# A decoder block in fp32 on one core: load order behind the gate products, and the combination of attention groups in four pieces

## The chip, the core and the metric

The kernel runs on one core of a Trainium2 chip. The core has five engines with instruction queues of their own: PE (matrix products), DVE and POOL (elementwise work), ACT (activation functions and copies), and SP, which here only issues transfers. ACT and POOL can issue transfers too. The metric is the device time of one execution in microseconds; lower is better. A profiled execution adds a trace of every instruction.

## The reference

The block computes, for x of 2048 tokens and 1024 channels:

```
h      = rmsnorm(x) * gain
proj   = h @ w_in                       # 5376 columns: q, k, v, u, z, gate_a, gate_b
y_attn = softmax-combination over 3 dilation groups of windowed attention (256 columns)
u, z   = gelu(proj_u), gelu(proj_z)     # 512 columns each
y_gmlp = u * (w_spatial @ layernorm(z) + b_spatial)      # per chunk of 128 tokens
merged = sigmoid(gate_a) * (y_attn @ w_branch_attn) + sigmoid(gate_b) * (y_gmlp @ w_branch_gmlp)
x      = x + rmsnorm(merged @ w_out)
x      = x + rmsnorm(relu(rmsnorm(x) @ w_mlp_in)**2 @ w_mlp_out)
```

The combination of the three attention groups, for each token and head, takes the running maxima and denominators of the groups, forms three weights that add to one, scales the three group outputs by them and adds them up.

## The kernel before

**Arithmetic.** Every fp32 operand of a large product is split into a rounded high part and a rest (`split`, L67), and one product is three matmuls: high by high, high by rest, rest by high (`mm3`, L94). The 2048 tokens are four chunks c of 512; half 0 is chunks 0 and 1, half 1 is chunks 2 and 3.

**Stages around the change.** After q, k and v have been computed and stored, a generator (`filler`, L761) supplies matrix products in small steps, and other work is laid between its steps. One step of a plain product is one `mm3` for one of eight slices of the contraction. The filler's queue is: u and z of half 1, the gates (`gates`, L664), then z of half 0. Gates and the rest of u are computed by a seven-product scheme over both halves. Its list `seq` has phases; a product is twelve matmuls in four steps. The last phase has ten products, for half 0, and starts at index LAST. Each product needs one piece of weights, loaded four products ahead (`piece`) and split by POOL three products ahead (`split_piece`); each result is stored to DRAM one product later (`out_`).

During the gates the 48 units of attention are laid between the steps. When they are through, 75 more steps of the gates remain. Between these steps lie the combinations of chunks 2 and 3; those of chunks 0 and 1 lie between the steps of z of half 0. `combine` (L955) is a generator: it loads the three groups' rows of a chunk (A for chunks 2 and 3; one buffer, cw, for chunks 0 and then 1), does the arithmetic on DVE and ACT, and then PE transposes the result (L990), ACT evacuates it (L993) and SP stores it to the DRAM tensor ya_d (L994). The calls `combined((steps, k), ...)` say how many steps of the filler pass before the next piece of combination k; k counts the chunks in the order 2, 3, 0, 1.

**z of half 0.** It reads hT_b0 and then hT_b1 (the normalised input of chunks 0 and 1, split, reloaded from DRAM by `reload_h`, eight loads each of 512 KB) and the two tiles w_z0 (reloaded from wz_d, four loads of 1024 KB, `want(5)`). One chunk is four blocks of tokens of eight steps each; ACT applies Gelu to each block (L572), DVE takes its statistics (L574), and at the end of a chunk normalises it (L579). The branch weights wb are six tiles, each loaded into one of two raw buffers, its high part split by POOL and its rest by DVE (`split_in`). `spatial` loads the spatial weights into memory that the gates' result tiles (ga) held.

**The merge.** After z the branch products start: `load_y(2)` loads the six operand tiles yt of chunk 2 (two from ya_d, four from yg_d) and POOL splits them; `early_gates` loads gate values and the first output weights; `merge` (L1139) runs, for each of eight column blocks, six and twelve matmuls into two banks, which DVE multiplies by the gates (L1153). The spatial products of chunks 0 and 1 (`sz_out`, L546) lie behind the first two column blocks. Then `out_block` multiplies by w_out.

**What sets the order.** PE's order is the program's. The order of the other engines is chosen when the kernel is built, by a planner that models the run and takes, for each engine, the ready instruction that comes first in the program. `behind()` (L175) pins what is written inside it behind the last instruction written so far on ACT, DVE, POOL and SP. At run time each queue is strictly in order: an instruction that waits holds all that stand behind it, transfers on SP included.

Two lists rule the places that matter here: in `gates`, `ins` holds loads, of which one is issued after each product; and in the last phase `reload_h(0)` is put into `ins`, while the loads of w_z0 are issued together at index LAST + 2:

```
            if t == LAST + 2:
                want(5)
            ...
            for _ in range(2 if half and i == 4 else 1):
                if ins:
                    sp.dma_start(*ins.pop(0))
```

The six branch weights are issued ahead of z of half 0, and hT_b1's eight loads together where z begins (L780).

Of the kernel before, what the change touches and what calls it, by code (L numbers as in the profile page):

```python
# [41 lines left out]
def block_kernel(ctx, tc, a, out):  # L42
# [100 lines left out]
    ya_d = dtile([2, P, S], "yad")  # L143
# [443 lines left out]
    def want(q):  # L587
        if q < len(queue) and q not in loaded:
            wi, kind, n, half = queue[q]
            if kind == "z":  # L590
                if half and not n:
                    loaded[q] = load_wide(wi, "w_z1")
                    for kk in range(2):
                        sp.dma_start(wz_d[kk], f32(loaded[q][kk]))
                elif not n:
                    loaded[q] = wide_tiles("w_z0")
                    for kk in range(2):
                        for o in range(2):
                            sp.dma_start(f32(loaded[q][kk])[:, o], wz_d[kk][:, o])
            else:  # L600
                loaded[q] = load_w(wi, f"w_{kind}{n}{half}")

# [61 lines left out]
    def gates():  # L664
# [12 lines left out]
        for t, (half, i, n) in enumerate(seq):  # L677
            if t in starts:
                ph, t0 = starts[t], t
                if ph + 1 < len(phases):  # L680
                    s = (ph + 1) % 2
                    if not slots[s]:
                        slots[s] = hp.tile([P, 2, 2, 4, 512], F32R, name="opA", tag="hT", bufs=2)
                    for j, i2 in enumerate(phases[ph + 1][1]):
                        new = operand(phases[ph + 1][0], i2, slots[s][:, j])
                        ins += new[0]
                        todo += new[1]
                else:
                    ins += reload_h(0)
            elif todo and (t - t0) % 3 == 1 and t > t0 + 1:  # L690
                w, k = todo.pop(0)
                with behind():
                    split(w[:, 0, k:k + 2], w[:, 1, k:k + 2], f32(w)[:, 1, k:k + 2], "act", "pool")
            if t == LAST + 2:
                want(5)
            piece(t + PIECES)
            split_piece(t + SPLITS)
            if i in (1, 6, 5, 4):
                bank[n] = psum_mm(f"g{half}{i}{n}")
            p, w, h = bank[n], g_["w"].pop(t), g_["b"][half, i]  # L700
            for k in range(4):
                for m, (l, r) in enumerate(((0, 0), (0, 1), (1, 0))):
                    pe.matmul(p, w[:, l, k], h[:, r, k], start=i in (1, 6, 5, 4) and not k and not m,  # L703
                              stop=k == 3 and m == 2, skip_group_check=True)
                if (t, k) == (3, 2) and late:
                    sz_out(*late.pop(0))
                yield
            if t == 3:
                a = [ga.tile([P, 512], F32, name=f"ga{n_}", tag=f"ga{n_}", bufs=1) for n_ in range(12)]
                xs += a[:7]  # L710
                zs += a[7:9]
                vs = a[9:11]
                g_["vs"] = vs + xs[8:] + zs[8:]
                g_["raws"] += a[11:] + vs + zs[8:]
            x, z, fn = xs[n], zs[n], AF.Copy if n < 8 else AF.Gelu_apprx_tanh
            while out_:
                sp.dma_start(*out_.pop())
            for _ in range(2 if half and i == 4 else 1):
                if ins:
                    sp.dma_start(*ins.pop(0))  # L720
            if i == 1:
                act.activation(x, p, AF.Copy)
            elif i == 2:
                act.activation(z, p, fn)
                o = z, 0, 0
            elif i == 6:
                dve.tensor_add(z, x, p)
            elif i == 7:
                dve.tensor_add(x, x, p)
            elif i == 5:  # L730
                if (half, n) == (0, 0):
                    g_["vs"] = a[9:11]
                v = g_["vs"].pop(0)
                g_["vs"].append(v)
                dve.tensor_add(v, x, p)  # L735
                o = v, 1, 1
            elif i == 3:
                dve.tensor_add(z, z, p)
                o = z, 0, 1
            else:  # L740
                dve.tensor_add(x, x, p)
                o = x, 1, 0
            if n > 7 and i in (5, 3, 4):
                act.activation(o[0], o[0], fn)
            if i in (2, 5, 3, 4):
                c, dst = 2 * half + o[2], gate_d if n < 8 else u_d
                out_.append((dst[n % 8 * 2 + o[1], :, c * 512:(c + 1) * 512], o[0]))
# [13 lines left out]
    def filler():  # L761

        for q, (wi, kind, n, half) in enumerate(queue):
            if kind == "z" and n == 1:
                continue
            if kind == "g":
                yield from gates()
                cw.append(wp.tile([P, 4096], F32, name="cw", tag="w", bufs=3))
                next(cs[2])
                continue  # L770
            want(q)
            if kind == "u":
                want(q + 1)
            if (kind, n) == ("u", 1):
# [1 line left out]
            w = loaded[q]  # L776
            if kind == "z":
                if not half:
                    for z in reload_h(1):
                        sp.dma_start(*z)  # L780
                for ci in range(2):
                    yield from paced(z_chunk(zps[half], w, half * 2 + ci))
                    if half and not ci:
                        gates_ahead()
                continue
# [6 lines left out]
                    sp.dma_start(u_d[n * 2 + m, :, c * 512:(c + 1) * 512], t)  # L792

    fill = filler()
    cw, cs = [], []

    def steps(n):
        for _ in range(n):
# [156 lines left out]
    def combine(c):  # L955
# [18 lines left out]
        dve.reciprocal(M, M)  # L974
        for g in range(3):
            dve.tensor_mul(E[:, :, g, :], E[:, :, g, :], M)
        for i in range(4):
            for j in range(4):
                o = A[:, i, 0, j * 64:(j + 1) * 64]
                act.activation(o, o, AF.Copy, scale=E[:, i, 0, j:j + 1])  # L980
        for g in range(1, 3):
            o = A[:, :, g, 0:256].rearrange("p i (j e) -> p i j e", j=4)
            dve.tensor_tensor(o, o, widen(E[:, :, g, :], 64), op=OP.mult)
        dve.tensor_add(A[:, :, 1, :256], A[:, :, 1, :256], A[:, :, 2, :256])
        dve.tensor_add(A[:, :, 0, :256], A[:, :, 0, :256], A[:, :, 1, :256])
        yield
        for m in range(2):
# [3 lines left out]
            yt = cb.tile([P, 512], F32, name=f"ya_{c}{m}", tag="cya", bufs=2) if c > 1 else \  # L991
                st.tile([P, 512], F32, name=f"ya_{c}{m}", tag="ev", bufs=3)
            act.activation(yt, pt, AF.Copy)  # L993
            sp.dma_start(ya_d[m, :, c * 512:(c + 1) * 512], yt)  # L994
        yield

    units = [(g, c, j) for g in range(3) for c in range(4) for j in range(4)]
# [53 lines left out]
            with behind():  # L1051
                next(cs[k])

    combined((0, 0), (4, 1), (16, 0), (18, 0), (0, 1), (20, 1))
    steps(75 - 58)
    ec.close()
    ega.close()

    e2r = ExitStack()
    wbp = stack(e2r, "wbp", 1, side="right")  # L1060
    wb = [wbp.tile([P, 2, D], F32R, name=f"wb{k}") for k in range(6)]
    for k in range(6):
        raw = wp.tile([P, D], F32, name=f"wbraw{k}", tag="raw", bufs=2)
        split_in(wb[k], a["w_branch"][:, k, :], raw)
    ez = ExitStack()
    zps[0] = stack(ez, "zp0", 1, side="right")
    sg = spatial(zps[0], 0)
    next(sg)
    combined((14, 2), (14, 2), (1, 3), (14, 3))
    steps(5)  # L1070
    next(sg)
    combined((10, 3))
    run(fill)
    e1.close()

# [966 lines left out]
```

## Time and profile before

| | |
|---|---|
| median of 3 runs | 2671.59 us (2671.57 to 2674.1) |
| the profiled execution | 2670.21 us |
| its span, first to last instruction | 2668.5 us |
| PE busy | 2622.1 us, 98% of the span |
| DVE, ACT, POOL busy | 1650.0, 1090.5, 1192.3 us |
| mean granted PE clock | 0.992 |
| z of half 0 on PE | from 1014.57 to 1076.5 us |
| first merge on PE | from 1076.5 to 1132.9 us |

How such rows are read. A timeline row is: start in us, duration in us, engine (SPq and ACTq are the queues as they issue transfers), source line, operation, output<-input by the program's names, shape, count, and in brackets the idle time before it with the engine or transfer that ended it. A wait row is: who waited, at which line, for whom: total us, times, longest us. A row of a stretch is: from:to, length, busy us and instruction count of PE, of PE's weight loads, of DVE, ACT and POOL, the granted PE clock, the mean busy share of the 16 transfer engines, and GB/s. A transfer row is: output<-input, queue, count, KB each, median us from issue to landing. Ends of matmuls are modelled; starts are what to go by.

### The profile page before, as it was taken

The numbers are of one execution on the slowest core, as the hardware profiler recorded it, in microseconds if no ns is written. First come the engines' busy times: TensorE is split into PE (matmuls) and PEld (weight loads), VectorE is DVE, ScalarE is ACT, GpSimd is POOL, SyncE is SP. The second block draws the span as 40 slices with busy tenths as digits, with TensorE's granted clock in tenths as the row PEclk, the third lists the DMA queues.
The fourth block names the chain that finished last, engine by engine and source line by source line (L and its number), as shares of the span: only waits on it lengthen the run. The fifth ranks groups of instructions, "written<-read, shape, count | busy, mean of one in ns | idle before, by whom it ended". The sixth has DMA issues, their size and how long they took to land. (4 is left out here: it accounts for less than half of the span.)

```text
span 2668.5 us, 35509 instructions
## 1 busy us (share of the span) xinstructions
PE 2622.1 (98%) x12458; PEld 2188.0 (82%) x12458; DVE 1650.0 (62%) x2793; ACT 1090.5 (41%) x2281; POOL 1192.3 (45%) x1089
## 2 busy tenths in 40 slices
PE   9999999999999997899999999999999999999998
PEld 8888888888888876688888888888888888888887
DVE  5676675534533454665676665655537888888866
ACT  5213111254455333344445545655545333233334
POOL 0363354375464542310233564223315776676645
PEclk9999999999999998899999999999999999999999
DMA  8779768988888887643666464653343212222235
GB/s 321 281 248 320 270 226 293 300 286 256 289 271 241 240 294 285 228 167 137 208 225 256 135 227 152 214 155 121 110 151 111 87 60 83 87 87 87 87 111 213
DMA packets 389284, 528.29 MB, mean 198 GB/s; under 512 B 57009, under 2 KB 242097, under 8 KB 387570
## 3 DMA queue, kind: packets, MB, share of 16 engines
q1 hardware_dynamic: 301488, 438.13, 49.5%
q0 software_dynamic: 14992, 51.65, 5.1%
q10 hardware_dynamic: 72626, 36.25, 4.5%
q8 instruction: 98, 1.61, 0.2%
q14 instruction: 80, 0.66, 0.1%
HBM read 342.77 MB, written 183.17 MB: 197 GB/s over the span
## 5 line engine op out<-in xcount | busy, mean ns | idle before, releaser
L1893 PE MATMUL ya<-T_spots,s 128*128 128x512 f32 x1176 | 289.2, 389 | 0.7 <-ACT T_spots L70 0.5
L70 ACT ACTIVATE s<-sraw 128x768 fp32r<-128x768 f32 (+1 forms) x184 | 127.2, 696 | 330.2 <-POOL sraw L1694 156.2
L1893 PEld LDWEIGHTS ya<-T_spots,s 128*128 128x128 f32 x1176 | 220.5, 188 | 47.3 <-ACT T_spots L70 0.9
L78 DVE TENSOR_TENSOR s<-sraw,s 128x512 fp32r<-128x512 f32 x172 | 184.4, 1097 | 8.6 <-ACT s L70 7.2
L1366 PE MATMUL aa<-B,A 128*128 128x512 f32 x768 | 182.4, 390 | 0.7 <-DVE A L85 0.7
L1337 POOL TENSOR_TENSOR s<-w1r 128x512 f32<-128x512 f32 x32 | 42.3, 1323 | 308.6 <-DVE S L78 271.0
L703 PE MATMUL g<-opA,spots 128*128 128x512 f32 x672 | 171.8, 400 | 2.5 <-DVE cv L735 2.5
L1366 PEld LDWEIGHTS aa<-B,A 128*128 128x128 f32 x768 | 143.8, 188 | 31.3 <-DVE A L85 1.1
L703 PE MATMUL g<-opB,spots 128*128 128x512 f32 x648 | 164.7, 398 | 1.7 <-POOL spots L78 1.0
L1893 PE MATMUL yc<-T_spots,s 128*128 128x512 f32 x624 | 159.6, 389 | 0.0
L95 PE MATMUL x<-hT_a,wq 128*128 128x512 f32 x384 | 149.7, 390 | 0.0
L96 PE MATMUL x<-hT_a,wq 128*128 128x512 f32 x384 | 149.4, 389 | 0.0
L97 PE MATMUL x<-hT_a,wq 128*128 128x512 f32 x384 | 149.4, 389 | 0.0
L703 PEld LDWEIGHTS g<-opA,spots 128*128 128x128 f32 x672 | 122.0, 190 | 25.0 <-issue 2.9
L78 POOL TENSOR_TENSOR spots<-gr,spots 128x512 fp32r<-128x512 f32 x98 | 128.1, 1310 | 23.0 <-PE g L703 8.3
L1893 PEld LDWEIGHTS yc<-T_spots,s 128*128 128x128 f32 x624 | 117.1, 188 | 24.3
L703 PEld LDWEIGHTS g<-opB,spots 128*128 128x128 f32 x648 | 117.0, 189 | 23.9 <-POOL spots L78 1.8
L70 ACT ACTIVATE hl<-r 128x512 fp32r<-128x512 f32 x48 | 30.4, 633 | 235.4 <-POOL r L321 89.0
L72 POOL TENSOR_SCALAR spots<-gr 128x512 fp32r<-128x512 f32 x86 | 53.9, 627 | 142.8 <-PE g L703 105.6
L951 DVE TENSOR_REDUCE o<-po 128x256 f32<-128x512 f32 x48 | 33.2, 691 | 132.5 <-PE po L950 132.5
L1693 POOL TENSOR_TENSOR sraw<-sraw 128x256 f32<-128x256 f32 x56 | 41.9, 748 | 161.4 <-DVE s L78 158.4
L78 POOL TENSOR_TENSOR T_spots<-w2r,T_spots 128x512 fp32r<-128x512 f32 x70 | 104.5, 1520 | 7.3 <-ACT T_spots L70 7.3
(422 smaller groups left out, 6959.6 us busy)
## 6 DMA issues: line engine op xcount, KB each, us to landing
w1r<-in_w_mlp_in_dram SPq DMA_DIRECT2D x64, 512.0 KB, 3.6
sraw<-sd SPq DMA_DIRECT2D x128, 256.0 KB, 3.2
qk<-hl SPq DMA_DIRECT2D x24, 1024.0 KB, 5.5
qq<-qk SPq DMA_DIRECT2D x96, 256.0 KB, 5.2
w2r<-in_w_mlp_out_dram SPq DMA_DIRECT2D x16, 1024.0 KB, 7.8
sd<-u ACTq DMA_DIRECT2D x63, 256.0 KB, 3.5
g<-gated SPq DMA_DIRECT2D x58, 256.0 KB, 3.9
gr<-sgd SPq DMA_DIRECT2D x53, 256.0 KB, 4.8
```

The lines of the kernel that those rows point to most:

```text
L70: act.activation(hi, src, AF.Copy)
L72: pool.tensor_scalar(hi, src, 1.0, 1.0, op0=OP.mult, op1=OP.mult)
L78: (pool if lo_eng == "pool" else dve).tensor_sub(lo, src, f32(hi))
L95: pe.matmul(ps, lh, rh, start=start, stop=False)
L96: pe.matmul(ps, lh, rl, start=False, stop=False)
L97: pe.matmul(ps, ll, rh, start=False, stop=stop)
L703: pe.matmul(p, w[:, l, k], h[:, r, k], start=i in (1, 6, 5, 4) and not k and not m, stop=k == 3 and m == 2, skip_group_check=True)
L951: dve.tensor_reduce(ot[:, :, j * 64:(j + 1) * 64], po.rearrange("p (b h e) -> p b e h", b=4, h=2), axis=AX.X, op=OP.add)
L1337: pool.tensor_add(s1, a21, a22)
L1366: pe.matmul(p, w[:, l, k, :], h[:, r, k, :], start=i in (1, 6, 5) and not k and not n, stop=k == 3 and n == 2, skip_group_check=True)
L1693: pool.tensor_add(a22, a21, a22)
L1893: pe.matmul(p, s[:, l], w[r], start=i in (1, 2, 5) and not m and not o, stop=m == 1 and o == 2, skip_group_check=True)
```

## The change

Six edits that belong together.

1. `want(5)` no longer issues the four loads of w_z0 but returns them. At the start of the last phase they are put into `ins` with the eight loads of hT_b0, in the order two of w_z0, four of hT_b0, two of w_z0, four of hT_b0. One is issued after each of the ten products, two after the second and the third.
2. `combine` yields twice more: loads; weights of the groups; scaling; sums; transposes, evacuation and store. The places of the pieces between the steps are written anew. Chunk 2's first arithmetic is at step 18 (20 before), its transposes at 36 (38); chunk 3's transposes at 56 (58).
3. The stores to ya_d are issued by ACT's queue, not SP's.
4. The branch weights are not issued ahead of z but one every sixth step in it, from the sixth to the thirty-sixth.
5. The eight loads of hT_b1 are put into a list, `zin`, and issued one per step from the start of z.
6. In z, the pieces of chunk 0's combination stand at steps 12, 14, 17 and 24 after the step in which cw's loads are written, those of chunk 1 at 24 (loads), 38, 40, 43 and 52. The preparation of the spatial weights' row sums stands at 48.

```diff
                 elif not n:
                     loaded[q] = wide_tiles("w_z0")
-                    for kk in range(2):
-                        for o in range(2):
-                            sp.dma_start(f32(loaded[q][kk])[:, o], wz_d[kk][:, o])
+                    return [(f32(loaded[q][kk])[:, o], wz_d[kk][:, o]) for kk in range(2) for o in range(2)]
...
                 else:
-                    ins += reload_h(0)
+                    ws, hs = want(5), reload_h(0)
+                    ins += ws[:2] + hs[:4] + ws[2:] + hs[4:]
...
-            if t == LAST + 2:
-                want(5)
...
-            for _ in range(2 if half and i == 4 else 1):
+            for _ in range(2 if half and i == 4 or t in (LAST + 1, LAST + 2) else 1):
...
             if kind == "g":
                 yield from gates()
+                want(q + 1)
                 cw.append(wp.tile([P, 4096], F32, name="cw", tag="w", bufs=3))
                 next(cs[2])
                 continue
-            want(q)
+            if q not in loaded:
+                want(q)
...
                 if not half:
-                    for z in reload_h(1):
-                        sp.dma_start(*z)
+                    zin.extend(reload_h(1))
...
         for g in range(3):
             dve.tensor_mul(E[:, :, g, :], E[:, :, g, :], M)
+        yield
         for i in range(4):
...
             dve.tensor_tensor(o, o, widen(E[:, :, g, :], 64), op=OP.mult)
+        yield
         dve.tensor_add(A[:, :, 1, :256], A[:, :, 1, :256], A[:, :, 2, :256])
...
             act.activation(yt, pt, AF.Copy)
-            sp.dma_start(ya_d[m, :, c * 512:(c + 1) * 512], yt)
+            act.dma_start(ya_d[m, :, c * 512:(c + 1) * 512], yt)
...
-    combined((0, 0), (4, 1), (16, 0), (18, 0), (0, 1), (20, 1))
-    steps(75 - 58)
+    combined((0, 0), (4, 1), (14, 0), (4, 0), (4, 0), (10, 0), (2, 1), (4, 1), (4, 1), (10, 1))
+    steps(75 - 56)
...
-    for k in range(6):
+
+    def load_wb(k):
         raw = wp.tile([P, D], F32, name=f"wbraw{k}", tag="raw", bufs=2)
         split_in(wb[k], a["w_branch"][:, k, :], raw)
...
     next(sg)
-    combined((14, 2), (14, 2), (1, 3), (14, 3))
-    steps(5)
-    next(sg)
-    combined((10, 3))
+    while not cw:
+        steps(1)
+    todo = {12: (2,), 14: (2,), 17: (2,), 24: (2, 3), 38: (3,), 40: (3,), 43: (3,), 52: (3,)}
+    for n in range(1, 54):
+        steps(1)
+        if zin:
+            sp.dma_start(*zin.pop(0))
+        if n % 6 == 0 and n <= 36:
+            load_wb(n // 6 - 1)
+        if n == 48:
+            next(sg)
+        for k in todo.get(n, ()):
+            combined((0, k))
     run(fill)
```

2 lines of the change are left out of this document (1 added, 1 removed).

## The prediction

> **What bounds the kernel now.** First the page's head, then what the matrix engine waits for in the stretch that the change touches.
>
> ```profile
> span 2668.5 us, 35509 instructions
> PE 2622.1 (98%) x12458; PEld 2188.0 (82%) x12458; DVE 1650.0 (62%) x2793; ACT 1090.5 (41%) x2281; POOL 1192.3 (45%) x1089
> ```
>
> PE is the bound, and only its pauses can be won: 46 us in all, and what runs slow behind them. The waits of PE from 950 to 1300 us:
>
> ```profile
> PE yt L990 <- issue: 13.7, 1, 13.7
> PE b L95 <- POOL yt L72: 3.3, 1, 3.3
> PE b L96 <- POOL yt L78: 2.9, 4, 1.3
> PE g L703 <- DVE cv L735: 2.5, 1, 2.5
> ...
> PE g L703 <- POOL spots L78: 1.0, 2, 0.6
> ...
> PE g L703 <- POOL spots L72: 0.8, 1, 0.8
> ```
>
> These six lines are 24.2 of the 46 us. The timeline of PE places them: the end of the gates, the z stage (1014.57 to 1076.5), the first merge (1076.5 to 1132.9).
>
> ```profile
> 978.58 4.48 PE L703 MATMUL g<-opA,spots 128*128 128x512 f32 x12 [2.52 <-DVE cv L735]
> 982.85 3.03 PE L703 MATMUL g<-opB,spots 128*128 128x512 f32 x12
> ...
> 1014.57 0.39 PE L95 MATMUL z<-w_z,hT_b 128*128 128x512 f32 x1
> 1014.80 0.39 PE L96 MATMUL z<-w_z,hT_b 128*128 128x512 f32 x1
> ...
> 1047.50 1.94 PE L990 MATMUL yt<-ident,cw 128*128 128x128 f32 x8 [13.73 <-issue]
> 1049.66 0.63 PE L96 MATMUL z<-w_z,hT_b 128*128 128x512 f32 x1
> 1050.09 0.63 PE L97 MATMUL z<-w_z,hT_b 128*128 128x512 f32 x1
> ...
> 1076.32 0.39 PE L97 MATMUL z<-w_z,hT_b 128*128 128x512 f32 x1
> 1080.02 0.79 PE L95 MATMUL b<-yt,wb 128*128 128x512 f32 x1 [3.31 <-POOL yt L72]
> ...
> 1092.22 5.42 PE L551 MATMUL sz<-wsp,z 128*128 128x128 f32 x32
> ...
> 1101.58 3.73 PE L551 MATMUL sz<-wsp,z 128*128 128x128 f32 x32
> ```
>
> A matmul normally starts 0.23 us after the last (1014.57, 1014.80); behind a pause it is 0.43 (1049.66, 1050.09). So a pause costs twice.
>
> **Part 1: the z stage.** Why are the transposes of chunk 0's combination (L990) late? SP's timeline, then DVE's first step with the third piece of cw:
>
> ```profile
> 1013.43 0.32 SPq L717 DMA_DIRECT2D ud<-ga  x1
> 1016.15 0.32 SPq L748 DMA_DIRECT2D ud<-ga  x1
> 1016.52 0.93 SPq L91 DMA_DIRECT2D wbraw<-in_w_branch_dram  x2
> ...
> 1019.87 0.42 SPq L530 DMA_DIRECT2D bsp<-in_b_spatial_dram  x1
> 1023.83 2.56 SPq L91 DMA_DIRECT2D wbraw<-in_w_branch_dram  x2
> 1026.44 0.98 SPq L960 DMA_DIRECT2D cw<-att  x2
> ...
> 1033.08 0.43 SPq L960 DMA_DIRECT2D cw<-att  x1
> 1033.56 5.02 SPq L780 DMA_DIRECT2D hT_b<-hbd  x8
> ```
>
> ```profile
> 1040.02 0.17 DVE L964 TENSOR_TENSOR M<-M,cw 128x16 f32<-128x16 f32 x1
> ```
>
> The six branch weights stand ahead of cw on SP, and from the third on each waits for one of two raw buffers to be split; so cw's last load leaves 18.5 us into the z stage. From its use to the transposes are 1047.50 - 1040.02 = 7.5 us. The new program writes cw's loads first, then hT_b's one per step, and a branch weight only at every sixth step, so cw stands behind the gates' last store (1016.15) and at most the four loads of the spatial weights (to 1020.29, three of them waiting in SP's order for stores of ga to land). Three issues of 0.5 bring the third to about 1021.3, 6.7 us into the stage. Landing times:
>
> ```profile
> cw<-att SPq DMA_DIRECT2D x3, 528.0 KB, 7.0
> ```
>
> 1021.3 + 7.0 + 7.5 = 1035.8, or 21.2 us into the stage; if the planner lets cw pass the spatial loads, 1017.5 + 7.0 + 7.5 = 1032.0, 17.4. PE reaches the transposes after 25 steps of three matmuls, 75 x 0.227 = 17.0 us. The new wait is 0.4 to 4.2; I take 3, nearer the program's order. Removed are 13.7, 0.8 of the slow transposes (1.6 us to the next matmul, where 0.8 is the rate) and six matmuls 0.2 too slow, 1.2: 15.7. Net gain 12.7. The rest of the part costs nothing: hT_b's eight loads of chunk 1 leave some 12 us earlier in the stage than the 19 of now and are due at step 33, 22 us in; the branch weights are needed only after 44 us; chunk 1's combination has 28 steps, 19 us, from its load to its transposes for 7.0 + 7.5. Without that cover each would be a wait of its own landing, about 7 us.
>
> By the Trainium skill (TensorE: Matmul & The Clock Gate, Part 1) the array's clock halves after an idle window of about 3.4 us and comes back after one of work. The matmuls behind the 13.73 agree, 0.43 against 0.23. By it a new wait of 3 would be free of this, and one of 4.2 would add 1.7 to its own 1.2: 2649.3 in place of the sum below.
>
> **Part 2: the end of the gates.** The combination of chunk 2 is now one block; DVE:
>
> ```profile
> 973.97 3.87 DVE L983 TENSOR_TENSOR A<-A,E 128x1024 f32<-128x1024 f32 x2
> ```
>
> The add L735 into cv that frees PE at 978.58 stands in order behind this 3.87 us of combination. Cut into statistics, products, sums and transposes four steps (2.7 us) apart and begun two steps sooner, this wait should go: 2.5, and the slow twelve matmuls behind it, 4.3 us where 2.7 is the rate: 4.1. Against it stands the order of loads. The last piece of hT_b0 now leaves with the last product, behind the store at 1013.43, about 1013.9. The landing of these loads, from the tile's view, and the stretch:
>
> ```profile
> DMA to landing us min/median/max: 4.5/7.4/11.5
> ```
>
> ```profile
> 988.00:1016.00 28.00, 26.26 (x118) 21.00 (x117) 12.37 (x22) 8.43 (x23) 9.54 (x10) 1.00 1.04 385
> ```
>
> z's first product wants it as its 21st matmul, 1014.57 + 20 x 0.227 = 1019.1. Landing at 1018.4 to 1025.4 it costs 0 to 6.3; I take the median, 2.2, less 0.2 for queues that now start sooner: 2.0. Net 2.1. The 1.8 of POOL's waits (spots) I leave: their pieces share the full transfers; an end of 0 or 3.6 for them goes into the range. The eight ya stores leave SP for ACT, where one issue costs 0.4; behind each pair stands z's or the gates' next evacuation, eight steps (5.4 us) apart on PE, so 0.8 of issue hides in ACT's pauses:
>
> ```profile
> L242 ACTq DMA_DIRECT2D hTd<-hr x16: 366/406/963, 216.1 to 281.5; - x16
> ```
>
> **Part 3: the first merge.** This is the part least seen in the change's words. SP before the merge, and its longest wait:
>
> ```profile
> 1072.84 1.05 SPq L994 DMA_DIRECT2D yad<-ya  x2
> 1073.97 0.91 SPq L91 DMA_DIRECT2D yt<-yad  x2
> ```
>
> ```profile
> SPq L994 <- ACT ya L993: 19.3, 2, 18.8
> ```
>
> ```profile
> 1060.00:1072.00 12.00, 12.00 (x54) 9.58 (x53) 9.32 (x27) 7.07 (x21) 0.00 (x0) 1.00 0.01 1
> ```
>
> SP stands 18.8 us at chunk 1's ya store with the transfers idle (1 GB/s), and the yt loads are queued behind it. They do not wait for the end of z: they leave at 1073.97 while z runs to 1076.5, and the compiled kernel places them in hT_b0's memory, last read by chunk 0. With the store on ACT's queue nothing late stands ahead of them, so they land, and POOL (idle then) splits them, inside z. What goes: the pause from z's last matmul (1076.32 + 0.23) to 1080.02, 3.5; the first 18 matmuls of b, 1080.02 to 1092.22, 12.2 where 18 x 0.227 = 4.1 is the rate, 8.1; the first sz, 5.4 where the second has 3.7, 1.7. Sum 13.3. What is late next is DVE:
>
> ```profile
> 1076.40:1132.90 56.50, 47.53 (x211) 37.56 (x209) 39.88 (x56) 21.08 (x31) 20.75 (x22) 0.85 0.71 253
> ```
>
> Its 39.9 us of work would have to fit in 56.5 - 13.3 = 43.2, beside loads of gates whose memory frees only at z's end. I let DVE pause 7.5 instead of 3.3 and give back 4.3: gain 9.0. Bounds: 0 (the loads still come late) and 13.3; that DVE fills most of the stage is the row nearest, so I stay below the upper end.
>
> **Sum.** The profiled execution took 2670.21 us (span 2668.5 and 1.7 around it), 1.4 under the median of 2671.59. 2670.2 - 12.7 - 2.1 - 9.0 = 2646.4.
>
> **Rivals.** (a) The merge gains nothing: the planner may put a gate's or a raw weight's load, whose buffer frees late, ahead of yt. For it: readiness in its own model orders SP. Against: no such load stands there now. 2655.4. (b) Chunk 0's sums are pinned behind z's second Gelu and its statistics, while ACT does the sixteen scalings first:
>
> ```profile
> 1042.21 3.93 ACT L980 ACTIVATE cw<-cw,E 128x64 f32<-128x64 f32 x16 [1.38 <-DVE E L976]
> ...
> 1050.09 1.28 ACT L572 ACT_TABLE_LOAD   x1
> ```
>
> In that order the table load (1.3), and by my estimate 1.3 for one more activation and z's statistics, come between the scalings and the sums, and the first of the two sums (1.2, a third of the DVE block above) no longer runs beside the scalings: about 3.8 more. On the later of the two landings that is a wait of 4.2 + 3.8 = 8.0, and 1.3 of slow clock (six matmuls 0.2 too slow each): 9.3 in place of 3, 2646.4 + 6.3 = 2652.7. (c) The transfers bound the gates' end: 988 to 1016 runs at a share of 1.04, so an earlier PE only finds later data. Then the last piece costs its full 6.3: gain 4.1 - 6.3, total 2650.7. The Trainium skill says as much (DMA: Bandwidth & Descriptors, Issuing engines are not separate DMA queues): a second issuing engine saves only issue time. The trace agrees on the full stretch, but the 1 GB/s row shows SP's waiting, not transfers, as the limit before the merge. (d) The written order has no effect on the planner: the branch weights pass cw as now. 2670.2 - 2.1 - 9.0 = 2659.1; if the merge stays too, 2668.1, no change. (e) Slower: the z operands (8 x 512 and 4 x 1024 KB, 8.4 MB), spread over ten products each behind a store, slip past the gates. All of it late is 8.4 MB at 385 GB/s, 21.8, and 7.4 to land: PE waits 29.2 at z's start, 2670.2 + 29.2 - 4.1 - 12.7 - 9.0 = 2673.6. It decides from a wait of about 25.8; against it, the planner issues a ready load on an idle SP ahead of its place: the first tile of w_z0, written in the third product of the last phase, leaves before that phase begins.
>
> **How the numbers follow.** Forecast 44 in 100, (a) 17, (b) 14, (c) 8, (d) 6 and 4, (e) 7. Under 0.2% (5.3 us) a measurement of this kernel hardly tells from no change. Faster 0.89, same 0.04, slower 0.07. The range: all best bounds together are 15.3 (15.7 less 0.4) + 5.9 (4.1 and 1.8) + 13.3 = 34.5, 2635.7; above, it reaches past (d) to 2660, leaving out no change, slower, and part of the tails.
>
> **What would show it.** Right: no 13.7 before L990, cw's three loads ahead of the branch weights, yt's loads before z ends, b starting within 0.5 us of z, no clock under 1 from 1040 to 1095. Wrong: a wait of 5 us or more at z's start or at L990, or yt's loads still behind something that waits for ACT.

## The result, and the profile after

The change made no difference that these runs can tell: 2675.9 us (median of 20) against 2673.94 us (median of 20), a ratio of 1.0007 with a 95% interval of 0.9999 to 1.0015. The prediction was 2646.4 us, and 2635.7 to 2660 as its range. It was wrong.

The profiled execution of the changed kernel took 2677.99 us (span 2676.0), that of the kernel before 2670.21. Most of these 7.8 us aren't the change's: up to the last product of attention all five queues hold the same instructions in the same order, and that product starts at 955.01 us in one execution and at 960.69 in the other. In the eleven edited kernels below, it starts between 955.4 and 964.2. So I measure from that product to the first product by w_out, and leave the time as a whole to the repeated runs.

The stretches before and after, the gates' end, z of half 0, and the merge, with the columns of the prediction (from:to, length, busy time of PE, weight loads, DVE, ACT, POOL, granted clock, transfer share, GB/s). First the kernel before:

```profile
955.00:1014.60 59.60, 55.34 (x244) 44.75 (x243) 30.30 (x55) 19.61 (x48) 22.07 (x22) 0.97 0.91 324
1014.60:1076.50 61.90, 48.17 (x211) 39.34 (x209) 31.15 (x71) 23.33 (x53) 10.06 (x10) 0.89 0.65 229
1076.50:1132.90 56.40, 47.43 (x210) 37.56 (x209) 39.88 (x56) 21.08 (x31) 20.75 (x22) 0.85 0.72 253
```

and then the changed kernel:

```profile
960.70:1015.20 54.50, 53.20 (x244) 43.64 (x243) 27.45 (x55) 17.45 (x46) 24.38 (x22) 1.00 0.97 338
1015.20:1095.70 80.50, 52.09 (x212) 41.81 (x211) 39.93 (x71) 22.16 (x52) 23.16 (x22) 0.81 0.60 210
1095.70:1138.30 42.60, 40.24 (x209) 33.88 (x207) 35.77 (x56) 21.41 (x31) 9.80 (x10) 1.00 0.86 290
```

The gates' end is 5.1 us shorter (2.1 predicted for it and the start of z together), the merge 13.8 shorter (9.0 predicted), and z is 18.6 longer where 12.7 less was predicted. The three add up to 0.3 us. Two of the prediction's three parts held or did better, and the third took all of it back. What PE waits for, from 940 to 1300 us:

```profile
PE yt L990 <- issue: 27.2, 2, 23.0
PE o L95 <- DVE g L1164: 2.1, 1, 2.1
PE z L97 <- DMA hT_b<-hbd: 1.2, 1, 1.2
PE o L95 <- ACT mg L70: 0.8, 1, 0.8
PE g L700 <- POOL spots L72: 0.7, 1, 0.7
PE g L700 <- POOL spots L78: 0.6, 1, 0.6
```

(Line numbers moved: L700 was L703, L1164 was L1153, L958 was L960.) The stall of 2.5 us on cv and the waits for POOL's yt are gone. The wait at the transposes, L990, has doubled, and it comes twice. PE's timeline shows where:

```profile
1021.34 0.50 PE L97 MATMUL z<-w_z,hT_b 128*128 128x512 f32 x1 [1.22 <-DMA hT_b<-hbd]
...
1057.09 1.94 PE L990 MATMUL yt<-ident,cw 128*128 128x128 f32 x8 [22.99 <-issue]
1058.68 0.78 PE L95 MATMUL z<-w_z,hT_b 128*128 128x512 f32 x1
1059.25 0.63 PE L96 MATMUL z<-w_z,hT_b 128*128 128x512 f32 x1
1059.68 0.63 PE L97 MATMUL z<-w_z,hT_b 128*128 128x512 f32 x1
...
1084.90 1.94 PE L990 MATMUL yt<-ident,cw 128*128 128x128 f32 x8 [4.20 <-issue]
...
1095.44 0.39 PE L97 MATMUL z<-w_z,hT_b 128*128 128x512 f32 x1
1095.67 0.39 PE L95 MATMUL b<-yt,wb 128*128 128x512 f32 x1
```

The last two lines are the good part: the merge's first product follows z's last in 0.23 us, at the full rate. The bad part is 22.99 us in front of chunk 0's transposes (13.73 before), and 4.20 in front of chunk 1's (none before). Behind both, matmuls come 0.43 us apart instead of 0.23. Of the 18.6 us that z is longer, 9.3 are the longer wait at chunk 0, 4.2 the wait at chunk 1 and 1.2 that for hT_b; by my estimate most of the rest is the slow matmuls behind the two long waits.

Why are chunk 0's transposes late? By the prediction cw's loads were the thing to look at. SP's timeline says that they went nearly as predicted:

```profile
1017.18 1.00 SPq L958 DMA_DIRECT2D cw<-att  x2
...
1023.33 0.43 SPq L958 DMA_DIRECT2D cw<-att  x1
1023.80 3.36 SPq L1077 DMA_DIRECT2D hT_b<-hbd  x6
1027.24 0.40 SPq L91 DMA_DIRECT2D wbraw<-in_w_branch_dram  x1
1028.72 1.54 SPq L1077 DMA_DIRECT2D hT_b<-hbd  x2
1031.20 8.96 SPq L91 DMA_DIRECT2D wbraw<-in_w_branch_dram  x2
```

The third load left 8.2 us into z (6.7 predicted). From cw's view, the loads issued from 1016 to 1024 landed after this long (7.0 predicted for the third):

```profile
DMA to landing us min/median/max: 5.4/6.2/7.2
```

So the data were there by 1030.5. DVE's timeline shows what it did then, and POOL's what DVE was waiting for:

```profile
1034.82 0.18 DVE L575 BATCH_NORM_AGGREGATE mv<-bs 128x2 f32<-128x6 f32 x1
1038.57 1.23 DVE L78 TENSOR_TENSOR wb<-wbraw,wb 128x1024 fp32r<-128x1024 f32 x1 [3.57 <-POOL wb L72]
1042.26 1.23 DVE L78 TENSOR_TENSOR wb<-wbraw,wb 128x1024 fp32r<-128x1024 f32 x1 [2.46 <-POOL wb L72]
1043.40 0.17 DVE L961 TENSOR_TENSOR M<-cw 128x16 f32<-128x16 f32 x1
```

```profile
1037.49 1.05 POOL L72 TENSOR_SCALAR wb<-wbraw 128x1024 fp32r<-128x1024 f32 x1 [10.86 <-DMA wbraw<-in_w_branch_dram]
1041.18 1.05 POOL L72 TENSOR_SCALAR wb<-wbraw 128x1024 fp32r<-128x1024 f32 x1 [2.64 <-DMA wbraw<-in_w_branch_dram]
```

DVE is idle and the data are in place, but two instructions stand first in its queue: the rests of branch weights 0 and 1 (L78). Their raw loads left behind hT_b's, so POOL had their high parts only at 1038.5 and 1042.2. The first step of chunk 0's combination, M, starts at 1043.40, 12.9 us after its data landed.

That suggested a theory, in terms of the code. In the loop over z's steps, `load_wb` is written ahead of the combination piece of the same step. At step 12 both occur: weight 1's split is written, and then M under `behind()`, which pins it behind the last instruction written on each queue. On DVE that is weight 1's rest. The rivals were that transfers crowd each other, and that the pin at step 12 is all there is to it.

### The profile page after: what moved, and what is told of

Same layout as the page of the kernel before. It is cut to its first block, busy times and chain, and to the rows that moved or that the text cites. A ratio compares the mean times of both kernels' runs of the same rounds, so it can differ in the third digit from the quotient of the medians.

```text
span 2676.0 us, 35501 instructions
## 1 busy us (share of the span) xinstructions
PE 2617.2 (98%) x12458; PEld 2185.3 (82%) x12458; DVE 1652.9 (62%) x2793; ACT 1087.0 (41%) x2278; POOL 1197.9 (45%) x1089
## 3 DMA queue, kind: packets, MB, share of 16 engines
q1 hardware_dynamic: 300336, 436.03, 49.6%
## 5 line engine op out<-in xcount | busy, mean ns | idle before, releaser
L78 DVE TENSOR_TENSOR s<-sraw,s 128x512 fp32r<-128x512 f32 x172 | 184.5, 1097 | 8.5 <-ACT s L70 7.2
L1348 POOL TENSOR_TENSOR s<-w1r 128x512 f32<-128x512 f32 x32 | 42.4, 1324 | 307.7 <-DVE S L78 261.0
L700 PE MATMUL g<-opA,spots 128*128 128x512 f32 x672 | 170.0, 397 | 0.0
L700 PE MATMUL g<-opB,spots 128*128 128x512 f32 x648 | 164.5, 398 | 1.3 <-POOL spots L72 0.7
L700 PEld LDWEIGHTS g<-opA,spots 128*128 128x128 f32 x672 | 121.2, 188 | 21.8
L78 POOL TENSOR_TENSOR spots<-gr,spots 128x512 fp32r<-128x512 f32 x98 | 127.7, 1307 | 22.3 <-PE g L700 8.3
L700 PEld LDWEIGHTS g<-opB,spots 128*128 128x128 f32 x648 | 116.7, 188 | 23.1 <-POOL spots L72 1.1
L78 POOL TENSOR_TENSOR T_spots<-w2r,T_spots 128x512 fp32r<-128x512 f32 x70 | 104.4, 1520 | 7.3 <-ACT T_spots L70 7.3
```

The lines of the kernel that those rows point to most:

```text
L78: (pool if lo_eng == "pool" else dve).tensor_sub(lo, src, f32(hi))
L1348: pool.tensor_add(s1, a21, a22)
```

## The experiments

In the table: the lengths of the three stretches in one profile of each kernel (gates from the last attention product to z's first product, merge up to the first product by w_out), their sum, and the ratio of the times to the kernel before with its 95% interval.

| kernel | gates | z | merge | sum | ratio |
|---|---|---|---|---|---|
| before | 59.6 | 61.9 | 56.4 | 177.9 | 1 |
| changed | 54.5 | 80.5 | 42.6 | 177.6 | 1.0007 (0.9999 to 1.0015) |
| e1_swap | 54.5 | 76.0 | 42.9 | 173.4 | 0.9988 (0.9978 to 0.9997) |
| e2_rest_pool | 54.8 | 65.1 | 43.0 | 162.9 | 0.9963 (0.9948 to 0.9977) |
| e3_before_act_stores | 59.4 | 64.0 | 43.3 | 166.7 | 0.9970 (0.9960 to 0.9981) |
| e4_after_sp_stores | 54.9 | 74.4 | 52.8 | 182.1 | 1.0014 (1.0005 to 1.0024) |
| e5_old_load_order | 62.6 | 76.4 | 42.8 | 181.8 | 1.0032 (1.0021 to 1.0044) |
| e6_rest_pool_order | 53.4 | 64.5 | 42.4 | 160.3 | 0.9961 (0.9948 to 0.9973) |
| e7_pool_busy | 54.8 | 85.0 | 49.6 | 189.4 | 1.0054 (1.0040 to 1.0069) |
| e8_mixed | 54.2 | 54.6 | 53.8 | 162.6 | 0.9945 (0.9933 to 0.9958) |
| e9_pinned_rests | 54.4 | 59.3 | 42.8 | 156.5 | 0.9918 (0.9905 to 0.9932) |
| e10_early_chunk1 | 54.3 | 62.5 | 43.1 | 159.9 | 0.9951 (0.9938 to 0.9963) |
| e11_rowsum_last | 54.1 | 57.0 | 43.2 | 154.3 | 0.9926 (0.9911 to 0.9941) |

**e1_swap: is it the pin?**

```diff
+        for k in todo.get(n, ()):
+            combined((0, k))
         if n % 6 == 0 and n <= 36:
             load_wb(n // 6 - 1)
         if n == 48:
             next(sg)
-        for k in todo.get(n, ()):
-            combined((0, k))
```

> The changed kernel with one edit: in the loop over z's steps the combination pieces are written ahead of the branch weight of the same step, not behind it (steps 12 and 24). Theory (pin): in the changed kernel chunk 0's first maximum M started at 1043.40, 13 us after its data landed (1023.33 + 7.2), because its pin is the last DVE instruction written before it, the rest of branch weight 1 (ended 1043.5), whose raw load went out at 1031.2 behind hT_b. With the swap the pin is z's statistics: M starts within 1 us of the landing of cw's third load, about 15 to 16 us into z (28.2 in the changed kernel). The first scaling of the sums still stands behind the rests of weights 0 and 1 on DVE, so the transposes come only about 5 us earlier: wait of PE at L990 about 18 instead of 23.0, time about 0.998 of the changed kernel's. Rival (transfers): cw and the weights are late because the loads crowd; then M stays near 28 us into z, or cw lands later, and the wait stays 23. Rival (the pin is all): the wait falls to 3 to 5 and the time by about 20 us.

DVE and then PE of this kernel, whose z starts at 1011.47:

```profile
1025.77 0.14 DVE L962 TENSOR_TENSOR M<-M,cw 128x16 f32<-128x16 f32 x1
...
1038.66 1.23 DVE L78 TENSOR_TENSOR wb<-wbraw,wb 128x1024 fp32r<-128x1024 f32 x1 [2.51 <-POOL wb L72]
1039.80 1.22 DVE L982 TENSOR_TENSOR cw<-cw,E 128x1024 f32<-128x1024 f32 x1
```

```profile
1049.65 1.94 PE L990 MATMUL yt<-ident,cw 128*128 128x128 f32 x8 [19.26 <-DVE cw L985]
```

The second step of M, the first that needs cw's third load, runs 14.3 us into z (28.4 in the changed kernel). So the pin held it. The wait fell by 3.7 us only, as the theory said and not as "the pin is all" would have it: the chain now stops half way, its first scaling on DVE (L982) still behind weight 1's rest. A pin moved is not enough; the rests have to be out of the way of the whole chain.

**e2_rest_pool: DVE's queue without the weights.**

```diff
-        split_in(wb[k], a["w_branch"][:, k, :], raw)
+        split_in(wb[k], a["w_branch"][:, k, :], raw, lo_eng="pool")
```

> The changed kernel with the rests of the six branch weights computed by POOL instead of DVE; order of pieces and weights as in the changed kernel. No branch weight is left in DVE's queue. Theory: DVE's queue alone holds chunk 0's combination, so M starts when cw's third load lands (15 to 16 us into z), the transposes come 7.5 us later, about 23 us into z, PE waits about 4 instead of 23.0, chunk 1's wait of 4.2 goes to under 1, z takes 54 to 57 us instead of 80.5, and the time falls by 22 to 26 us, to about 0.991 of the kernel before. Rival (transfers): the wait at L990 stays above 12, time within 8 us of the changed kernel. Rival (POOL late): six rests of about 2.6 us on POOL delay yt's split, and a wait of 3 us or more for POOL returns at the first merge.

```profile
1034.38 1.06 PE L990 MATMUL yt<-ident,cw 128*128 128x128 f32 x8 [2.85 <-issue]
...
1067.91 1.94 PE L990 MATMUL yt<-ident,cw 128*128 128x128 f32 x8 [12.50 <-issue]
```

Chunk 0's wait is 2.85 us; the prediction had taken 3. The transfers are the same as in the changed kernel, so crowding alone did not cause the 23. It has a part in it: in the changed kernel weight 0's raw load left at 1027.24, behind six loads of hT_b, and POOL could start on it only at 1037.49. DVE's queue handed that delay on to the combination. Chunk 1's wait, though, rose from 4.2 to 12.5, so of the 20.1 us gained at chunk 0 8.3 were lost again. z takes 65.1 us where 54 to 57 were expected, and the ratio is 0.9963 where about 0.991 was. The expected end of chunk 1's wait was a miss; e6 and e7 take it up.

**e3_before_act_stores and e4_after_sp_stores: the stores to ya_d alone.** The first is the kernel before with

```diff
-            sp.dma_start(ya_d[m, :, c * 512:(c + 1) * 512], yt)
+            act.dma_start(ya_d[m, :, c * 512:(c + 1) * 512], yt)
```

and the second is the changed kernel with this line turned back.

> The kernel before with one edit: the stores to ya_d are issued by ACT's queue. Theory of part 3: yt's loads no longer stand behind chunk 1's store on SP; they land inside z, the pause of 3.3 us at b's first product and the slow matmuls behind it go, the merge takes 43 to 47 us instead of 56.4, time lower by 9 to 14 us (ratio 0.995 to 0.9965). The wait of 13.7 at L990 stays within 2 us. Rival: the merge's gain in the changed kernel (13.7) came from the moved branch weights and hT_b loads or from z's lengthening, which gave the loads time; then this kernel gains under 3 us.

> The changed kernel with the stores to ya_d back on SP's queue. Theory of part 3: yt's loads stand behind chunk 1's stores again, and in this program those come late (chunk 1's transposes at 70 us into z), so b waits 3 us or more for POOL, runs slow, and the merge takes 53 us or more instead of 42.7: time 9 to 14 us above the changed kernel (ratio to the kernel before about 1.005). Rival: no difference, because z is so long that all loads are done anyway.

The merge of the first, and of the second:

```profile
1087.60:1130.90 43.30, 40.33 (x210) 33.97 (x208) 35.29 (x56) 21.94 (x31) 9.79 (x10) 1.00 0.87 296
```

```profile
1084.70:1137.50 52.80, 45.45 (x210) 35.87 (x209) 41.01 (x56) 21.09 (x31) 20.87 (x22) 0.90 0.74 254
```

In both programs this one line decides the merge: 56.4 to 43.3 in the old one, 52.8 to 42.6 in the new. The rival, that other edits gave the loads their time, falls. But z pays: in the first it is 2.1 us longer (and chunk 1's transposes wait 1.72 us), in the second the kernel with ACT's stores has a z of 80.5 against 74.4 and a wait of 4.20 against none. So the store line is worth 11 us of the sum in the old program and 4.5 in the new one; between e4 and the changed kernel the intervals of the ratios overlap. The 9 to 14 us of time that were expected for each were too much: in the old program it is 6.5 in the medians (2666.78 against 2673.3), and in the new one no difference can be told.

**e5_old_load_order: what shortens the gates?** The changed kernel with w_z0's four loads together at LAST + 2 and hT_b's behind them, as before:

```diff
-                    ws, hs = want(5), reload_h(0)
-                    ins += ws[:2] + hs[:4] + ws[2:] + hs[4:]
+                    ins += reload_h(0)
...
+            if t == LAST + 2:
+                for o in want(5):
+                    sp.dma_start(*o)
...
-            for _ in range(2 if half and i == 4 or t in (LAST + 1, LAST + 2) else 1):
+            for _ in range(2 if half and i == 4 else 1):
```

> The changed kernel with the loads of the last phase in the order of the kernel before: w_z0's four issued together two products into the phase, then hT_b's eight one per product. The pieces of the combinations stay as changed. Theory of part 2: the gates' gain (last attention product to z's start 59.6 us before, 54.5 changed) comes from the pieces, that is from the 2.5 us stall on cv and the slow matmuls behind it, so 4.1 of the 5.1 stay: 54.5 to 55.5 us; the wait of 1.2 for hT_b at z's start goes; waits for POOL's spots stay between 1 and 2 us. Total within 1.5 us of the changed kernel. Rival: the order of the loads carries the gain; then the gates take 57 us or more.

A wait of PE, and POOL's row behind it:

```profile
PE g L702 <- POOL spots L72: 6.7, 1, 6.7
```

```profile
1005.88 0.62 POOL L72 TENSOR_SCALAR spots<-ga 128x512 fp32r<-128x512 f32 x1 [15.99 <-DMA ga<-sgd]
```

The theory was wrong. The stall on cv stayed away, as it has to when the pieces are finer, but the gates took 62.6 us: PE came earlier to a piece of weights that landed later, behind w_z0's 3 MB. The transfers of this kernel, from 975 to 985 and from 995 to 1005 us:

```profile
975.00:985.00 10.00, 10.00 (x50) 8.38 (x49) 5.64 (x10) 4.02 (x10) 8.63 (x7) 1.00 0.55 164
...
995.00:1005.00 10.00, 4.81 (x26) 3.72 (x24) 2.65 (x4) 2.37 (x3) 0.00 (x0) 0.85 1.03 409
```

Their share is 0.55 first, when there was room, and 1.03 twenty microseconds later, when PE stood. So the finer pieces take the stall away, but with the old order of loads the gates are 3.0 us longer than before; with the written order, which gets the data there in time, they are 5.1 shorter. What the written order would do with the old pieces no run shows.

**e6_rest_pool_order and e7_pool_busy: why is chunk 1 late?** e6 has the swap of e1, POOL's rests of e2, and cw's loads ahead of the spatial weights':

```diff
-    sg = spatial(zps[0], 0)
-    next(sg)
     while not cw:
         steps(1)
+    sg = spatial(zps[0], 0)
+    next(sg)
```

e7 is e4, where POOL idles in z's second half, with work for POOL that nobody needs (the rest of weight 5, nine times more, the same values):

```diff
+        if n == 38:
+            for _ in range(9):
+                pool.tensor_sub(wb[5][:, 1], raw5, f32(wb[5][:, 0]))
```

> Three edits to the changed kernel together: rests of the branch weights on POOL, combination pieces written ahead of the weight of the same step, cw's loads written ahead of the spatial weights' loads. With POOL's rests alone chunk 0's wait fell to 2.9 us, but chunk 1's grew to 12.5, by my reading since chunk 1's loads of cw are pinned on SP behind branch weight 3 (step 24), whose raw buffer POOL frees late. Theory: with the swap they stand ahead of weight 3 and leave about 41 to 43 us after the last attention product's z start minus 15, that is about 26 to 28 us into z; chunk 1's wait is 2 to 8; cw's third load of chunk 0 leaves about 3 us into z and chunk 0's wait is under 1. z takes 50 to 57 us, merge 43 to 48, ratio to the kernel before 0.989 to 0.993. Rival: chunk 1's wait was POOL's slowing of DVE, not SP's order; then it stays above 9 and the ratio above 0.994.

> The changed kernel with the ya_d stores on SP (POOL idle in the second half of z), and POOL made busy there: it computes the rest of branch weight 5 nine more times, the same values, which nobody needs sooner. Nothing else differs in any queue. Theory (DVE and POOL slow each other): in the changed kernel the same DVE instructions of chunk 1 took 3.50 (4 x L579), 2.17 (L984), 2.02 (L985) us beside POOL's split of yt, and 1.92, 1.23, 1.22 with POOL idle; here they take the long times again wherever POOL's nine lie beside them, and chunk 1's transposes come late by 2 to 5 us. Rival (the long times belong to transfers or to ACT): they stay at 1.92, 1.23 and 1.22.

In e6 cw's loads for chunk 1 left 25.2 us into z and chunk 0's wait fell to 0.43, but chunk 1 still waited 13.47: SP's order was not its cause, and the result is the rival's. e7 tests the rival alone. POOL's nine, and groups of DVE's instructions from 1058 to 1079 us (line, engine, operation, output<-input, shapes, count, busy us and mean ns):

```profile
1057.42 22.17 POOL L1083 TENSOR_TENSOR wb<-wbraw,wb 128x1024 fp32r<-128x1024 f32 x9 [2.29 <-DVE wb L78]
```

```profile
L104 DVE TENSOR_SCALAR v_ln<-mv 128x4 f32<-128x4 f32 x1 | 2.4, 2366 | 0.0
L112 DVE TENSOR_SCALAR t_ln<-t_ln 128x4 f32<-128x4 f32 x1 | 2.2, 2241 | 0.0
L110 DVE TENSOR_TENSOR t_ln<-r_ln 128x4 f32<-128x4 f32 x1 | 2.2, 2178 | 0.0
...
L574 DVE BATCH_NORM_STATS2 bs<-z 128x6 f32<-128x512 f32 x1 | 0.7, 682 | 0.0
...
L111 DVE TENSOR_TENSOR t_ln<-t_ln,v_ln 128x4 f32<-128x4 f32 x1 | 0.2, 161 | 0.0
```

and the same instructions in e4, with POOL idle:

```profile
L574 DVE BATCH_NORM_STATS2 bs<-z 128x6 f32<-128x512 f32 x2 | 1.3, 662 | 0.0
...
L104 DVE TENSOR_SCALAR v_ln<-mv 128x4 f32<-128x4 f32 x1 | 0.2, 171 | 0.0
L112 DVE TENSOR_SCALAR t_ln<-t_ln 128x4 f32<-128x4 f32 x1 | 0.2, 170 | 0.0
L110 DVE TENSOR_TENSOR t_ln<-r_ln 128x4 f32<-128x4 f32 x1 | 0.2, 161 | 0.0
```

DVE's order is the same in both; POOL's nine are the only addition. A DVE instruction of 0.17 us takes up to 2.4, about one of POOL's (22.17 / 9 = 2.46), and chunk 1's wait goes from none to 8.80 us, more than the 2 to 5 expected. The sums (L984, L985), which I expected long, ran after POOL had ended and took their 1.2. The same is seen where POOL's work is part of the program. The first line is of e6, beside POOL's rests; the second of the changed kernel, beside yt's split; the third of e4, with POOL idle:

```profile
1040.23 2.26 DVE L112 TENSOR_SCALAR t_ln<-t_ln 128x4 f32<-128x4 f32 x1
```

```profile
1072.22 1.85 DVE L969 TENSOR_TENSOR Z<-E,cw 128x16 f32<-128x16 f32 x3
```

```profile
1067.46 0.34 DVE L969 TENSOR_TENSOR Z<-E,cw 128x16 f32<-128x16 f32 x3
```

So a branch weight's rest on POOL (e2, e6) and yt's split inside z (the changed kernel) are paid for by DVE's chain of small steps. How much of the 12.5 and 13.47 us is due to this no run separates.

**e8_mixed, e9_pinned_rests, e10_early_chunk1, e11_rowsum_last: a version that beats both.** All have cw's loads ahead of the spatial weights'. They differ in where a branch weight is loaded, and where its rest is computed. e8 writes the weights in pairs behind the pieces:

```diff
-        split_in(wb[k], a["w_branch"][:, k, :], raw)
+        split_in(wb[k], a["w_branch"][:, k, :], raw, lo_eng="pool" if k in (2, 3) else "dve")
...
+        for k in {24: (0, 1), 36: (2, 3), 52: (4, 5)}.get(n, ()):
+            load_wb(k)
```

e9 loads weights 0 and 1 right behind cw and separates a weight's load from its rest, which is pinned behind a piece that is already written:

```diff
+    def rest_wb(k):
+        with behind():
+            dve.tensor_sub(wb[k][:, 1], raws[k], f32(wb[k][:, 0]))
...
+    load_wb(0)
+    load_wb(1)
+    sg = spatial(zps[0], 0)
+    next(sg)
...
+    rests = {17: (0, 1), 30: (2, 3), 46: (4, 5)}
+    loads = {24: (2, 3), 30: (4, 5)}
```

e10 is e9 without `behind()` for the rests, with rests at 24, 36 and 50, loads at 24 and 36, and chunk 1's pieces at 31, 33, 36 and 50. e11 is e9 with `if n == 53` for `if n == 48` (the row sums).

> A proposal: the changed kernel with cw's loads ahead of the spatial weights' loads, the branch weights written in pairs behind the combination pieces of steps 24, 36 and 52, weights 2 and 3 with their rests on POOL, the others on DVE. Theory: no branch weight stands ahead of chunk 0's chain or of chunk 1's loads; chunk 0's wait under 1, chunk 1's 0 to 5, z 48 to 53 us, merge 43 to 47, ratio 0.987 to 0.991. Rival: the weights come late instead, b's products wait for wb at the merge, merge above 48 and ratio above 0.992.

> A second proposal: cw's loads first, branch weights 0 and 1 loaded right behind them (ahead of hT_b), weights 2 and 3 after step 24, 4 and 5 after step 30; high parts on POOL as before, rests on DVE, each pair pinned behind a combination piece already written (steps 17, 30, 46). Theory: no weight stands ahead of a combination piece before it has landed, and POOL does only six high parts of 1.05 us and, from about 35 us into z, the split of yt. Chunk 0's wait under 1.5, chunk 1's 0 to 5 (two rests of 1.2 and the slowing by POOL's yt lie in its chain), z 48 to 53 us, merge 42.5 to 47, ratio 0.986 to 0.991. Rival: weights 4 and 5 hold yt's loads back on SP as in the first proposal, POOL's yt comes late and the merge takes over 50; ratio above 0.9925.

> A third proposal: as the second, but the rests are not pinned (the planner puts 0 and 1 into chunk 0's chain, 2 and 3 into chunk 1's), weights 4 and 5 come after step 36, and chunk 1's pieces stand at 31, 33, 36 and 50. Theory: two rests of 1.2 in chunk 0's chain cost a wait of 1 to 3 there, chunk 1 is no earlier since its data land at 27 us into z and the normalisation of chunk 0 lies there too: wait 0 to 5; yt's loads stand behind weights 4 and 5, whose buffers come free after chunk 1's rests, so the merge waits for POOL: 46 to 53. Ratio 0.989 to 0.994.

> The second proposal (pinned rests, ratio 0.9918) with the spatial weights' row sums at step 53 instead of 48. There chunk 1's weights of the groups (L974) stood on DVE behind L539, which waited 1.85 us for PE's row sums, and behind the rest of branch weight 3, from 1049.2 to 1052.5. Theory: chunk 1's chain gets 2 to 3.3 us shorter and its wait of 6.7 falls to 3.5 to 5; ratio 0.990 to 0.9915. Rival: chunk 1 is held by the landing of weight 3 and the wait stays within 0.7 of 6.7.

e8 has the shortest z, 54.6 (48 to 53 expected). Its rival's numbers came true, a merge above 48 and a ratio above 0.992, but by another way: not wb is late but yt, whose loads stand behind the last weights' on SP, so that the merge waits for POOL again.

```profile
PE b L96 <- POOL yt L78: 4.7, 5, 1.7
```

e9 keeps the merge at 42.8 and z at 59.3, and is 0.8% faster than the kernel before: 2651.29 us against 2673.53. Its waits at L990:

```profile
PE yt L990 <- issue: 8.3, 2, 6.7
```

They are 1.68 and 6.67 us, where under 1.5 and 0 to 5 were expected; z (48 to 53 expected) and the time (0.986 to 0.991) are over their ranges too. In e10 the unpinned rests went into chunk 0's chain, and it waited 4.64 us there (1 to 3 expected) and 5.89 at chunk 1 (0 to 5 expected); the merge stayed at 43.1, better than expected, and the ratio came out above its range of 0.989 to 0.994. e11 shortened chunk 1's wait to 5.12, by 1.55 where 1.7 to 3.2 was expected, and z by 2.3 to 57.0; its ratio is above the range given (0.990 to 0.9915), and its time can't be told from e9's.

## Why the prediction was wrong, step by step

**Part 1 failed, and its miss is larger than the whole error.** The step was "1021.3 + 7.0 + 7.5 = 1035.8, or 21.2 us into the stage". The transposes came 41.9 us into z, 20.7 later. The third load was 1.5 later (8.2 instead of 6.7) and its landing at most 0.2; the rest is on DVE. The chain began 12.9 us after the landing, and then took 13.7 us (1043.40 to 1057.09) instead of 7.5, with three more rests of weights (1.2 each, one with a wait of 0.9) and a slower scaling and sum among its steps. I had followed the branch weights on SP only, and priced them at nothing because they "are needed only after 44 us". That is when PE needs them. On DVE they have a place in a queue, which I never looked up: at the steps 12 and 24, weight and piece coincide, and the pin fell behind the weight. e2 shows that the other terms of this sum were nearly right: with the rests out of DVE's queue the transposes come 21.8 us into z, where 21.2 was worked out. That the wait is 2.85 there, where 3 was taken, is partly luck: 3 was picked between 0.4 and 4.2, and the 4.2 that goes with 21.2 became less because PE reached the transposes 19.0 us into z instead of 17.0, 1.2 of that by the wait for hT_b.

The claim that chunk 1 is covered by "28 steps, 19 us" failed too: there was a wait of 4.20 us. Chunk 1's chain, from M to the last sum, took 19.9 us beside POOL's split of yt; in e4, with yt split later, it took 12.7 and there was no wait. The 7.5 taken over from chunk 0 was too short even so, since z's normalisation of chunk 0 lies among the steps of this chain.

**Part 2 was right in its main term, low in its sum and incomplete in its cause.** The stall on cv is gone, with its slow matmuls, for which 4.1 was predicted, and the waits for POOL's spots fell from 1.8 to 1.3; the gates gained 5.1. The wait for hT_b is 1.22 (2.0 taken), so the net is about 3.9 where 2.1 was forecast. I had counted the order of loads as a cost only. e5 shows that without the new order the finer pieces lose 3.0 us: rival (c), an earlier PE that finds later data, is real in that kernel, and the new order prevents it.

**Part 3 was right in mechanism and too small.** 13.8 us instead of 9.0, over the upper end of 13.3; e3 gives 13.1 for the one line in the old program. The term of 4.3 that I gave back to DVE was wrong: I took DVE's 39.9 us of work in the merge as fixed. The same 56 instructions take 35.8 us when POOL's yt isn't beside them. The other half of that coin I missed: the split of yt now slows DVE inside z. z is 2.1 us longer in e3 than in the kernel before, and 6.1 longer in the changed kernel than in e4 (80.5 against 74.4).

**Rivals.** (b) had the place, chunk 0's sums pinned behind something late, but named z's statistics, worth 6 us; it was the weights' rests, worth 20. (a), (d) and (e) didn't happen: yt's loads left 30 us before z's end, cw's loads stood ahead of the weights, and z's operands came 1.2 us late. "No change" had 4 in 100, for the case that the written order does nothing; here it did much, in both directions, and the sum came out at zero. The reason to doubt was in the diff: the prediction worked out what `behind()` pins for z's statistics, but not for the two lines in front of the call.

By the Trainium skill (TensorE: Matmul & The Clock Gate, Part 1), quoted in the prediction, an idle window of about 3.4 us halves the array's clock. At the transposes the traces agree: behind waits of 2.85 (e2) and 1.68 (e9) us, eight transposes took 1.06 and 1.07 us; behind 4.20 and 22.99 they took 1.94. Elsewhere they don't. In the kernel before, the pause of 2.52 us on cv was followed by twelve matmuls in 4.27 us, 0.36 each, with a granted clock of 0.50 from 980 to 983 us. In e2, a pause of 1.95 us ahead of the first product by w_out (1120.70) was followed by matmuls 0.43 us apart, with 0.50 from 1123 to 1125. So the length of a pause alone doesn't decide it in these traces, and the prediction's step that a wait of 3 "would be free of this" held at e2's 2.85 without being safe.

## What to carry to other kernels

An operation that isn't needed for a long time still costs what stands behind it: for each piece of work that is moved or spread out, find its place on every in-order queue that it uses, and what comes next there, not only on the queue that loads it. Where an order is pinned "behind what was last written", read which line that is at each call. Work taken off one engine to save time in one stage lands in another, and there it has to be asked whom it slows: here POOL's split, moved into z, slowed DVE's chain of small steps there, and z gave back more than half of what the merge had gained (6.1 of 10.2 us, e4 against the changed kernel).

## What the hardware showed that was not expected

DVE and POOL hold each other up, by nearly a whole instruction of the other. Beside POOL's subtractions of 128x1024 (2.46 us each), DVE instructions on 128x4 elements took 2.18 to 2.37 us instead of 0.16 to 0.17, while others between them (L111, 0.161) and the statistics (L574, 0.682 and 0.662) took their usual time. The Trainium skill (SBUF — State Buffer, Who interferes with whom) describes this: the two engines share a pair of ports, which is locked for a whole instruction, and DVE instructions with one input outside certain modes are free of it. The trace agrees on the size of the delay and on the statistics. Which instructions are held up isn't settled by these runs: two of the slow ones (L104, L112) have one input, and whether they ran in such a mode no run shows; two with two inputs (L111, L113) were not slowed. The loss goes both ways: in the changed kernel POOL's last two subtractions of yt took 4.44 us together, and the two in the middle 2.56.

What stays open: against the kernel before, e2 and e6 are 15 and 18 us shorter in the stretch shown, but only 10 and 9 in the medians of the times. One profile each can't say how much of the difference is the variation of the earlier part, which is about 9 us between executions of the same instructions.
